# Rounding the narrow SBUF tiles of a float32 transformer kernel up to whole lines of 64 bytes

## Chip, core and metric

The kernel runs on one core of a Trainium2 chip. The metric is the device time of one execution in microseconds.

## The reference

Two blocks of two layers each run over one sequence of 512 tokens with 1024 features, all in float32. The first block is a Fox attention layer (16 heads of 64, a forget gate as a bias) and an MLA attention layer (16 heads, low-rank queries, keys and values), each followed by a gated FFN with a short convolution. The second block is an NSA layer (compressed, selected and window attention, with a multiscale pool beside them) and a conformer convolution of 31 taps, each followed by a SwiGLU FFN. A norm stands ahead of each layer, a residual after it.

```python
def conv_ffn(h, w_in, conv_w, conv_b, w_out):
    u = h @ w_in                                   # 1024 -> 2 * 2816
    u = conv_b + sum(up[:, j:j + s_len] * conv_w[j] for j in range(CONV_W))
    gate, val = jnp.split(u, 2, axis=-1)
    return (jax.nn.silu(gate) * val) @ w_out       # 2816 -> 1024

def first_block(x, ...):
    for layer in range(DEPTH):
        x = x + (fox_mixer(...) if layer < N_A else mla_mixer(...))
        x = x + conv_ffn(rmsnorm(x, ffn_norm[layer]), ...)
    return rmsnorm(x, final_norm)

def second_block(x, ...):
    for layer in range(DEPTH):
        h = rmsnorm_2(x, mix_norm[layer])
        x = x + (nsa_pool_mixer(h, ...) if layer % 2 == 0 else conformer_conv(h, ...))
        x = x + swiglu(rmsnorm_2(x, ffn_norm[layer]), ...)
    return rmsnorm_2(x, final_norm)
```

## The kernel before

Activations lie with features on the partitions and the 512 tokens along the free axis, in chunks of 128 features. The tensor engine multiplies in `float32r`, which keeps only part of a float32, so every factor is split into `hi` and `lo` (`split`, L300): ScalarE writes `hi`, VectorE the rest. A product is then three matmuls, hi with hi, lo with hi and hi with lo (`mm3`, L320 to L323). Most have 128 stationary columns of weights and stream 512 tokens.

Weights are loaded by `load` (L307): 512 KB or less into a `raw` tile of 1024 floats per partition, split at once into tiles `hi` and `lo`; each of the three has three buffers in the pool `wp`. The operand that streams past the weights is `xs` (the split input of a stage, `xsh` and `xsl`, which the MLA also uses for its heads' output), or `hh`/`hl` (the hidden layer of an FFN), `qlh`/`qll` and `lath`/`latl` (the latents of the MLA), `xkh`/`xkl` (a second split input of the MLA), `oh`/`ol` (the heads' output in Fox and NSA) and `poh`/`pol` (the pool's output).

A gated FFN (`ffn`, L692) has two halves: 44 tiles that stream `xs` against `w_in`, and 8 tiles with 22 chunks each that stream `hh` and `hl` against `w_out`. There are four of these. In the attentions a pipeline over heads (`pipeline`, L549) is mixed with projections that are drawn from a queue of generators (`_Fill`). The conformer gives its 31 taps to TensorE, VectorE and GpSimd.

Tiles are allocated from pools that stand one after another in a partition's memory: `cp` (constants: `vecs`, `ident`, `ones`, `gg`, `mhalf`), `wp` (weights), `xp` (`x`, `xs`), `tp` (temporaries, among them `var` twice and `m2`), `rp` (`rt` twice, `r`), and then, each from the same address, the pools of the stages. A stage's pool is released tile by tile, and a later tile waits for those that lay at its place. Tiles are placed in the order in which they are asked for, and each takes a whole number of units of 32 bytes per partition: a tile of 4 floats (`NQ`), such as `var`, takes one unit.

Of the kernel before, what the change touches and what calls it, by code (L numbers as in the profile page):

```python
# [17 lines left out]
P = 128  # L18
T = 512
# [21 lines left out]
def _blocks(w, col_sets):  # L41
    """[K, M] -> [blocks, 128, K/128 * cols]: one contiguous piece for each load."""
    k = w.shape[0] // P
    r = w.reshape(k, P, w.shape[1])
    return np.ascontiguousarray(
        np.stack([r[:, :, c].transpose(1, 0, 2).reshape(P, -1) for c in col_sets])
    )
# [12 lines left out]
def _lay_out(i):  # L60
    """Only layout of the inputs, and constants of the shapes."""
# [147 lines left out]
class _Fill:  # L209
    """Tensor engine work that may stand between the steps of an attention, in order."""  # L210
# [7 lines left out]
    def push(self, name, gen, at=None, gate=None):  # L218
        """gate: (step of the heads, how many heads must be past it), for tiles that are used again."""
        self.q.insert(len(self.q) if at is None else at, (name, gen, gate))  # L220
# [22 lines left out]
    def need(self, name):  # L243
        """The task of this name, to its end."""
        for task in [t for t in self.q if t[0] == name]:
            self._all(task[1])
            self.q.remove(task)
# [7 lines left out]
def _body(ctx, tc, a, out):  # L255
# [14 lines left out]

    nvec = a["vecs"].shape[1]
    vecs = cp.tile([P, nvec], F32, name="vecs")
# [15 lines left out]
    gg = cp.tile([P, NC8], F32, name="gg")  # L288
    G.memset(ones, 1.0)
    mhalf = cp.tile([P, NQ], F32, name="mhalf")  # L290
# [9 lines left out]
    def split(hi, lo, src, scale=None):  # L300
        """hi + lo is src (times scale) to float32's precision; each is exact in float32r."""
        if scale is None:
            return S.copy(hi, src), V.tensor_sub(lo, src, bc(hi))  # L303
        return (S.activation(hi, src, AF.Copy, scale=scale),
                V.scalar_tensor_tensor(lo, src, scale, bc(hi), op0=OP.mult, op1=OP.subtract))  # L305
# [19 lines left out]
    def mm2(acc, w, rh, rl, first, last):  # L325
        """w: hi and lo beside each other, 64 columns each; their products are added by join()."""
        PE.matmul(acc, w, rh, start=first, stop=False)
        PE.matmul(acc, w, rl, start=False, stop=last)
# [8 lines left out]
    def lin(acc, w, act, ks, cols, first=True, last=True, w0=0):  # L337
        """acc[cols, tokens] += sum over the chunks ks of w[k][:, cols].T @ act[k]."""
        wh, wl = w
        ah, al = act  # L340
        for n, k in enumerate(ks):
            mm3(acc, wh[:, k - w0, cols], wl[:, k - w0, cols], ah[:, k], al[:, k],
                first and n == 0, last and n == len(ks) - 1)
            yield STEP
# [8 lines left out]
    class Stats:  # L353
        """Sum over features of squares, gathered chunk by chunk."""
# [26 lines left out]
    def rsqrt(dst, src, n, eps):  # L381
        v = tp.tile([P, NQ], F32, name="var", tag="var", bufs=2)
        V.tensor_scalar(v, src, 1.0 / n, eps, op0=OP.mult, op1=OP.add)
        G.tensor_tensor(dst, v, mhalf, op=OP.pow)

    def wide(r):
        """[128 tokens, 4] -> the same for every partition, [128, 512]."""
        pr = bank("pr")
        for i in range(NQ):
            PE.transpose(pr[:, sl(i)], r[:, i : i + 1].to_broadcast([P, P]), ident)  # L390
        return pr
# [6 lines left out]
    class Norm:  # L398
        """Reciprocal root mean square of the tokens. What is made of it waits until the tensor
        engine has other work in hand: evictions that need it are put off by after()."""  # L400
# [7 lines left out]
        def step(self):  # L408
            if self.t is None:
                self.t = self.pool.tile([P, NQ], F32, name=self.name + "t", tag=self.name + "t", bufs=2)  # L410
                self.square(self.t)
            elif self.b is None:
                self.b = spread(self.t, self.pool, self.name)
                for f in self.put_off:
                    f()
                self.put_off = []
# [4 lines left out]
        def tick(self):  # L421
            """A tile of products has been queued."""
            self.left -= 1
            if self.left <= 0:
                self.step()
# [16 lines left out]
    def split_x(gname, dst=None, st=None, square_on=None):  # L442
        """x times its gain, as hi and lo."""
        dst = dst or xs
        for c in range(NC8):
            last = split(dst[0][:, c], dst[1][:, c], x[:, c], vec(gname, c))
            if st is not None:
                st.add(x[:, c], square_on)
        return last
# [9 lines left out]
    def out_proj(name, act, nk, per, blocks, b0=0, k0=0, late=False):  # L459
        """x += act @ weights; with late, the last chunk of act comes in after all others."""  # L460
        ah, al = [z[:, k0 : k0 + nk] for z in act]
        for b in range(0, blocks, 2):
            tiles = []
            for bb in (b, b + 1):
                w = load(a[name][b0 + bb], nk)
                for m in range(per):
                    tiles.append((bank(), w, sl(m), bb * per + m))
                    if not late:
                        acc = tiles[-1][0]
                        yield from lin(acc, w, (ah, al), range(nk), sl(m))  # L470
                        add_x(bb * per + m, acc)
            if late:
                for ks in (range(nk - 1), range(nk - 1, nk)):
                    for acc, w, cols, m in tiles:
                        yield from lin(acc, w, (ah, al), ks, cols, ks[0] == 0, ks[-1] == nk - 1)
                        if ks[-1] == nk - 1:
                            add_x(m, acc)
# [3 lines left out]
    def stack_q(f, s, name, pool):  # L481
        """Head s of a pair: hi in its own half of the partitions, lo in the other half."""
# [5 lines left out]
    def stack_k(f, s, ka, kl):  # L488
        """hi in both halves of ka, lo in the own half of kl."""
        S.copy(ka[own[s]], f[own[s]])  # L490
        V.tensor_copy(ka[own[1 - s]], f[own[s]])
        V.tensor_sub(kl[own[s]], f[own[s]], bc(ka[own[s]]))

    class Head:
        """Softmax attention of one head in three steps: scores, transposes, values."""
# [4 lines left out]
        def scores(self):  # L500
            pool = self.pool
            nm = pool.tile([P, NQ], F32, name="nm", tag="nm", bufs=3)
            sm = pool.tile([P, NQ], F32, name="sm", tag="sm", bufs=3)
# [10 lines left out]
            rc = pool.tile([P, NQ], F32, name="rc", tag="rc", bufs=3)  # L514
# [34 lines left out]
    def pipeline(prep, n, fill, edge):  # L549
        """Heads in a pipeline, with other work of the tensor engine between their steps."""  # L550
# [21 lines left out]
    # ------------------------------------------------------------------ Fox  # L572
    def fox():
        with ExitStack() as es:
# [27 lines left out]
            def forget():  # L602
# [4 lines left out]
                # softplus(z) with z = -logit: max(z, 0) + ln(1 + exp(-|z|))  # L607
# [83 lines left out]
    # ------------------------------------------------------------- gated FFN  # L691
# [44 lines left out]
    # ------------------------------------------------------------------ MLA  # L736
# [158 lines left out]
    # ------------------------------------------------------------------ NSA  # L895
    def nsa():
        with ExitStack() as es:
# [10 lines left out]
            ccmp = kp.tile([P, NQ * 32 + NQ], F32, name="ccmp")  # L908
# [9 lines left out]
            # two norms in a row: of x, and of what comes of it  # L918
# [8 lines left out]
            r1 = kp.tile([P, NQ], F32, name="r1")  # L927

            def square(t):
                rsqrt(r1, st1.sums(), D, EPS)  # L930
                m2 = tp.tile([P, NQ], F32, name="m2", tag="m2")
# [12 lines left out]
            with phase("n_x") as pool:  # L944
                # compressed keys and values
# [160 lines left out]
            # compressed branch  # L1106
# [82 lines left out]
    # ------------------------------------------------------------ conformer  # L1189
    def conformer():  # L1190
        with ExitStack() as es:
# [9 lines left out]
            with phase("c_x") as pool:  # L1201
# [3 lines left out]
                wdh = pool.tile([P, nw], F32R, name="wdh")  # L1205
                wdl = pool.tile([P, nw], F32, name="wdl")
# [3 lines left out]
                def conv(j, z, on, n_pe):  # L1210
                    """31 taps of chunk j: the first n_pe by the tensor engine, the rest by vector or gpsimd."""
                    y = zc[:, j]
                    if n_pe:
                        zh = pool.tile([P, T + 30], F32R, name="zh", tag="zh", bufs=2)
                        zl = pool.tile([P, T + 30], F32R, name="zl", tag="zl", bufs=2)
# [14 lines left out]
                # layer norm: sums about the mean of three chunks, and the exact shift from it  # L1230
# [88 lines left out]
                def beside(gen):  # L1319
                    """Tensor engine work, with the others' share of the convolutions beside it."""  # L1320
# [35 lines left out]
            rt = pool.tile([P, NQ], F32, name="lnt")  # L1356
            dt = pool.tile([P, NQ], F32, name="lndt")
            d2 = pool.tile([P, NQ], F32, name="lnd2")
# [30 lines left out]
    def final(gname):  # L1389
# [11 lines left out]
        rt = rp.tile([P, NQ], F32, name="rt", tag="rt", bufs=2)  # L1401
# [39 lines left out]
```

## Time and profile before

| | |
|---|---|
| time, median of 3 runs | 2606.76 us (2606.7 to 2606.8) |
| span of the profiled execution | 2603.5 us, 31317 instructions |
| granted clock of TensorE, mean over the span | 0.985 |
| HBM traffic | 83 GB/s over the span |

The span reaches from the first to the last instruction; the run's time also holds what lies around it, 3.3 us by the median. Matmuls are pipelined, so one starts before the one ahead of it ends: the time that a matmul costs in a stream is the distance from one start to the next, which the timeline shows, and not its own duration. Names stand without buffer numbers: `acc<-hh,hi` is a matmul into the accumulator `acc` that streams `hh` against the weights `hi`.

### The profile page before, as it was taken

Reading aid. Unit: us, or ns where it says so; the run is one execution under the profiler, and the core shown is the slowest. Engines: PE = TensorE matmul, PEld = TensorE weight load, DVE = VectorE, ACT = ScalarE, POOL = GpSimd, SP = SyncE. Lnnn points to the kernel's source line nnn. Section 1 sums busy time; section 2 is a strip of 40 time slices with the busy share of each in tenths; the row PEclk is TensorE's granted clock in tenths of the full one; section 3 lists DMA queues with packets and bytes.
Section 4 is the critical chain, followed back from the end, with each engine's and each line's share of the span. In section 5 each row is a group of like instructions: output and inputs, shape, how many; then the busy total and the mean of one; then the engine's idle time right before and its main releaser. Section 6 shows DMA issues by size and latency. Waiting matters only on the chain. (4 is left out here: it accounts for less than half of the span.)

```text
span 2603.5 us, 31317 instructions
## 1 busy us (share of the span) xinstructions
PE 2526.1 (97%) x11903; PEld 2088.6 (80%) x11903; DVE 1627.3 (63%) x2495; ACT 1140.7 (44%) x1933; POOL 464.8 (18%) x369
## 2 busy tenths in 40 slices
PE   8999999999999999999999999999999778999998
PEld 6988888888888888888888888888887546888886
DVE  7887777625677656777436996444328996544422
ACT  4664444324566544444324684222225453333221
POOL 3452000001132212000011222000004763100001
PEclk9999999999999999999999999999999988999999
DMA  4122333333311222333333212333332101333332
GB/s 150 58 66 68 103 97 97 91 97 102 88 57 55 72 73 83 102 96 95 93 93 117 64 51 84 97 97 96 89 100 73 57 17 33 99 97 97 93 97 69
DMA packets 65447, 218.90 MB, mean 84 GB/s; under 512 B 7536, under 2 KB 8560, under 8 KB 65296
## 3 DMA queue, kind: packets, MB, share of 16 engines
q1 hardware_dynamic: 65296, 216.90, 27.1%
q8 instruction: 93, 1.52, 0.3%
q14 instruction: 58, 0.48, 0.1%
HBM read 214.70 MB, written 2.10 MB: 83 GB/s over the span
## 5 line engine op out<-in xcount | busy, mean ns | idle before, releaser
L303 ACT CAST hi<-raw 128x1024 fp32r<-128x1024 f32 (+4 forms) x417 | 420.5, 1010 | 919.5 <-PE acc L322 716.2
L323 PE MATMUL acc<-xsh,lo 128*128 128x512 f32 x1792 | 700.3, 391 | 15.7 <-DVE lo L303 15.7
L321 PE MATMUL acc<-xsh,hi 128*128 128x512 f32 x1792 | 699.6, 392 | 3.0 <-ACT xsh L303 2.9
L303 DVE TENSOR_TENSOR lo<-raw,hi 128x1024 fp32r<-128x1024 f32 (+4 forms) x417 | 499.8, 1199 | 322.8 <-ACT hi L303 317.7
L322 PE MATMUL acc<-xsl,hi 128*128 128x512 f32 x1792 | 700.5, 391 | 0.8 <-DVE xsl L305 0.8
L323 PEld LDWEIGHTS acc<-xsh,lo 128*128 128x128 f32 x1792 | 338.2, 189 | 88.9 <-DVE lo L303 18.7
L321 PEld LDWEIGHTS acc<-xsh,hi 128*128 128x128 f32 x1792 | 338.2, 189 | 73.6 <-ACT xsh L303 3.3
L322 PEld LDWEIGHTS acc<-xsl,hi 128*128 128x128 f32 x1792 | 338.0, 189 | 73.1 <-DVE xsl L305 2.1
L373 POOL TENSOR_TENSOR ssum<-ssum,sq 128x512 f32<-128x512 f32 x75 | 120.4, 1609 | 1482.3 <-ACT sq L367 1472.3
L321 PE MATMUL acc<-hh,hi 128*128 128x512 f32 x704 | 279.1, 396 | 0.0
L322 PE MATMUL acc<-hl,hi 128*128 128x512 f32 x704 | 279.1, 396 | 0.0
L323 PE MATMUL acc<-hh,lo 128*128 128x512 f32 x704 | 279.1, 396 | 0.0
L522 POOL TENSOR_SCALAR lg<-lg,rc 128x384 f32<-128x384 f32 (+3 forms) x144 | 165.8, 1167 | 384.2 <-DVE rc L515 300.6
L710 DVE TENSOR_TENSOR y<-acc,r 128x512 f32<-128x512 f32 x88 | 60.4, 691 | 219.7 <-PE acc L323 219.5
L457 DVE TENSOR_TENSOR x<-x,acc 128x512 f32<-128x512 f32 x104 | 70.6, 685 | 158.6 <-PE acc L323 158.3
L323 PEld LDWEIGHTS acc<-hh,lo 128*128 128x128 f32 x704 | 132.6, 188 | 32.3
L322 PEld LDWEIGHTS acc<-hl,hi 128*128 128x128 f32 x704 | 132.6, 188 | 32.3
L321 PEld LDWEIGHTS acc<-hh,hi 128*128 128x128 f32 x704 | 132.6, 188 | 32.3
L1285 POOL TENSOR_TENSOR zc<-zc,pr 128x496 f32<-128x496 f32 (+17 forms) x79 | 127.0, 1611 | 65.2 <-ACT pr L1281 56.7
L707 DVE SCALAR_TENSOR_TENSOR y<-u,vecs,y 128x510 f32<-128x510 f32 (+1 forms) x176 | 130.9, 748 | 3.4 <-ACT y L705 0.6
L512 ACT ACTIVATE lg<-lg,nm 128x128 f32<-128x128 f32 x192 | 107.1, 560 | 47.2 <-DVE nm L510 46.3
L303 ACT CAST hh<-y 128x512 fp32r<-128x512 f32 x88 | 54.6, 621 | 135.6 <-DVE y L714 135.6
(366 smaller groups left out, 3843.1 us busy)
## 6 DMA issues: line engine op xcount, KB each, us to landing
raw<-in_ffn_in SPq DMA_DIRECT2D x88, 512.0 KB
raw<-in_swi_in SPq DMA_DIRECT2D x88, 512.0 KB
raw<-in_ffn_out SPq DMA_DIRECT2D x32, 448.0 KB
raw<-in_swi_out SPq DMA_DIRECT2D x32, 448.0 KB
raw<-in_pw SPq DMA_DIRECT2D x24, 512.0 KB
raw<-in_fox_qk SPq DMA_DIRECT2D x16, 512.0 KB
raw<-in_ffn_out SPq DMA_DIRECT2D x16, 512.0 KB
raw<-in_uqk SPq DMA_DIRECT2D x16, 512.0 KB
```

Source lines behind the costliest of these rows:

```text
L303: return S.copy(hi, src), V.tensor_sub(lo, src, bc(hi))
L321: PE.matmul(acc, lh, rh, start=first, stop=False)
L322: PE.matmul(acc, lh, rl, start=False, stop=False)
L323: last_mm[0] = PE.matmul(acc, ll, rh, start=False, stop=last).ins
L373: (sum_on or G).tensor_add(self.s, self.s, sq)
L457: V.tensor_add(x[:, c], x[:, c], acc)
L512: S.activation(lg, lg, AF.Exp, bias=nm[:, i : i + 1], scale=-1.0, accum_out=sm[:, i : i + 1])
L522: (V if i in self.on_v else G).tensor_scalar(self.p[i], self.p[i], rc[:, i : i + 1], None, op0=OP.mult)
L707: V.scalar_tensor_tensor(y[:, sh:], u[:, : T - sh], vec(f"cw{l}{2 - sh}", jj), y[:, sh:], op0=OP.mult, op1=OP.add)
L710: V.tensor_mul(y, acc, norm.b)
L1285: G.tensor_add(y[:, sh:], y[:, sh:], pr[:, sh:])
```

## The change

A helper `narrow` allocates a tile whose width is rounded up to a multiple of 16 floats and hands out the part that is used. All tiles of 4 or 8 floats and the others whose width isn't a multiple of 16 are allocated by it. Instructions, loops and transfers stay the same. Comments and docstrings are also blanked; after the new helper all lines stand 4 lower.

```diff
+    def narrow(pool, n, dt=F32, **kw):
+        return pool.tile([P, -(-n // 16) * 16], dt, **kw)[:, :n]
...
-    vecs = cp.tile([P, nvec], F32, name="vecs")
+    vecs = narrow(cp, nvec, name="vecs")
...
-    gg = cp.tile([P, NC8], F32, name="gg")
+    gg = narrow(cp, NC8, name="gg")
-    mhalf = cp.tile([P, NQ], F32, name="mhalf")
+    mhalf = narrow(cp, NQ, name="mhalf")
...
-        v = tp.tile([P, NQ], F32, name="var", tag="var", bufs=2)
+        v = narrow(tp, NQ, name="var", tag="var", bufs=2)
...
-                self.t = self.pool.tile([P, NQ], F32, name=self.name + "t", tag=self.name + "t", bufs=2)
+                self.t = narrow(self.pool, NQ, name=self.name + "t", tag=self.name + "t", bufs=2)
...
-            nm = pool.tile([P, NQ], F32, name="nm", tag="nm", bufs=3)
-            sm = pool.tile([P, NQ], F32, name="sm", tag="sm", bufs=3)
+            nm = narrow(pool, NQ, name="nm", tag="nm", bufs=3)
+            sm = narrow(pool, NQ, name="sm", tag="sm", bufs=3)
...
-            rc = pool.tile([P, NQ], F32, name="rc", tag="rc", bufs=3)
+            rc = narrow(pool, NQ, name="rc", tag="rc", bufs=3)
...
-            ccmp = kp.tile([P, NQ * 32 + NQ], F32, name="ccmp")
+            ccmp = narrow(kp, NQ * 32 + NQ, name="ccmp")
...
-            r1 = kp.tile([P, NQ], F32, name="r1")
+            r1 = narrow(kp, NQ, name="r1")
...
-                m2 = tp.tile([P, NQ], F32, name="m2", tag="m2")
+                m2 = narrow(tp, NQ, name="m2", tag="m2")
...
-                wdh = pool.tile([P, nw], F32R, name="wdh")
-                wdl = pool.tile([P, nw], F32, name="wdl")
+                wdh = narrow(pool, nw, F32R, name="wdh")
+                wdl = narrow(pool, nw, name="wdl")
...
-                        zh = pool.tile([P, T + 30], F32R, name="zh", tag="zh", bufs=2)
-                        zl = pool.tile([P, T + 30], F32R, name="zl", tag="zl", bufs=2)
+                        zh = narrow(pool, T + 30, F32R, name="zh", tag="zh", bufs=2)
+                        zl = narrow(pool, T + 30, F32R, name="zl", tag="zl", bufs=2)
...
-            rt = pool.tile([P, NQ], F32, name="lnt")
-            dt = pool.tile([P, NQ], F32, name="lndt")
-            d2 = pool.tile([P, NQ], F32, name="lnd2")
+            rt = narrow(pool, NQ, name="lnt")
+            dt = narrow(pool, NQ, name="lndt")
+            d2 = narrow(pool, NQ, name="lnd2")
...
-        rt = rp.tile([P, NQ], F32, name="rt", tag="rt", bufs=2)
+        rt = narrow(rp, NQ, name="rt", tag="rt", bufs=2)
```

## Rows read from the trace of the kernel before

**Rows 1.** The page, busy us of each engine (share of the span) xinstructions

```profile
PE 2526.1 (97%) x11903; PEld 2088.6 (80%) x11903; DVE 1627.3 (63%) x2495; ACT 1140.7 (44%) x1933; POOL 464.8 (18%) x369
```

**Rows 2.** Windows: stretch, its us, busy us by engine, granted clock, DMA

```profile
256.00:496.00 240.00, 240.00 (x1066) 198.82 (x1065) 177.91 (x224) 111.49 (x139) 8.54 (x5) 1.00 0.31 97
496.00:622.00 126.00, 126.00 (x540) 101.35 (x539) 41.06 (x45) 34.87 (x43) 10.12 (x8) 1.00 0.33 95
...
700.00:960.00 260.00, 260.00 (x1421) 225.47 (x1420) 179.76 (x375) 148.54 (x322) 64.85 (x60) 1.00 0.21 65
...
1962.00:2168.00 206.00, 158.08 (x599) 119.45 (x597) 198.81 (x232) 106.23 (x198) 129.09 (x82) 0.89 0.13 42
```

**Rows 3.** Timeline of PE, an FFN's first half: start us, duration us, what

```profile
299.81 0.39 PE L323 MATMUL acc<-xsh,lo 128*128 128x512 f32 x1
...
301.85 0.39 PE L323 MATMUL acc<-xsh,lo 128*128 128x512 f32 x1
```

**Rows 4.** Timeline of PE, an FFN's second half

```profile
539.64 0.39 PE L322 MATMUL acc<-hl,hi 128*128 128x512 f32 x1
...
542.92 0.39 PE L321 MATMUL acc<-hh,hi 128*128 128x512 f32 x1
```

**Rows 5.** Timeline of PE, the MLA's low-rank projections

```profile
652.52 0.39 PE L322 MATMUL acc<-xsl,hi 128*128 128x512 f32 x1
...
655.01 0.40 PE L321 MATMUL acc<-xkh,hi 128*128 128x512 f32 x1
...
656.88 0.40 PE L323 MATMUL acc<-xkh,lo 128*128 128x512 f32 x1
```

**Rows 6.** Timeline of PE, MLA attention, an output projection that streams xs

```profile
864.79 0.39 PE L323 MATMUL acc<-xsh,lo 128*128 128x512 f32 x1
...
870.68 0.40 PE L321 MATMUL pq<-qlh,hi 128*128 128x512 f32 x1
```

**Rows 7.** Timeline of PE, MLA, a query projection that streams ql

```profile
673.11 0.40 PE L321 MATMUL pq<-qlh,hi 128*128 128x512 f32 x1
...
677.33 0.95 PE L378 MATMUL pst<-ones,ssum 128*128 128x1 f32 x8
```

**Rows 8.** Groups by line, engine, operation and shape, of PE: xcount, busy us, mean ns

```profile
L322 PE MATMUL acc<-xsl,hi 128*128 128x512 f32 x1792 | 700.5, 391 | 0.8 <-DVE xsl L305 0.8
...
L321 PE MATMUL acc<-hh,hi 128*128 128x512 f32 x704 | 279.1, 396 | 0.0
...
L321 PE MATMUL pq<-qlh,hi 128*128 128x512 f32 x144 | 58.3, 405 | 0.0
...
L321 PE MATMUL acc<-oh,hi 128*128 128x512 f32 x96 | 38.0, 401 | 0.2 <-DVE nm L510 0.2
```

**Rows 9.** Waits, whole span: who waited for whom, us, times, longest

```profile
ACT hi L303 <- PE acc L322: 716.2, 262, 9.4
```

**Rows 10.** Timeline of PE, an FFN's first half after an interruption

```profile
268.46 0.40 PE L322 MATMUL acc<-xsl,hi 128*128 128x512 f32 x1
...
270.54 0.39 PE L322 MATMUL acc<-xsl,hi 128*128 128x512 f32 x1
```

**Rows 11.** Timeline of PE, MLA, values from lat, 256 columns

```profile
684.25 0.28 PE L321 MATMUL pv<-hi,lath 128*128 128x256 f32 x1
...
687.12 0.40 PE L321 MATMUL pq<-qlh,hi 128*128 128x512 f32 x1
```

**Rows 12.** Timeline of PE, Fox, values from xs, 256 columns

```profile
30.77 0.28 PE L322 MATMUL pv<-lo,xsh 128*128 128x256 f32 x1
...
34.13 0.28 PE L322 MATMUL pv<-lo,xsh 128*128 128x256 f32 x1
```

**Rows 13.** Groups by line of DVE: x is aligned, y is not

```profile
L457 DVE TENSOR_TENSOR x<-x,acc 128x512 f32<-128x512 f32 x104 | 70.6, 685 | 158.6 <-PE acc L323 158.3
L710 DVE TENSOR_TENSOR y<-acc,r 128x512 f32<-128x512 f32 x88 | 60.4, 691 | 219.7 <-PE acc L323 219.5
```

## Prediction

> **What bounds the kernel now.** I read the page's busy line first. The tensor engine is busy for 97% of the span, far ahead of the others [rows 1]. I then cut the span by stage with the table of windows. In a gated FFN's first half (256 to 496 us), in its second half (496 to 622) and in the MLA attention (700 to 960) the tensor engine is busy for the whole window, so what its matmuls save there moves the end. In the conformer (1962 to 2168) it is busy for 158 of 206 us and the vector engine for 199; there the vector engine sets the pace [rows 2].
>
> A matmul's own duration says little here, since matmuls overlap. What counts is the distance from one start to the next, and the timeline gives it. In the middle of an FFN's first half ten rows in a row go from 299.81 to 301.85, nine distances of 226.7 ns [rows 3]. In its second half fifteen rows go from 539.64 to 542.92, fourteen distances of 234.3 ns [rows 4]. Both are 128x512, with weights from the same buffers, at a granted clock of 1.00, the higher of its two levels [rows 2]; nothing idles between them. The difference is 7.6 ns, 3%.
>
> What differs is the streamed operand. The addresses in the program of before follow from its allocations: every tile takes whole units of 32 bytes per partition. The weights (`raw`, `hi`, `lo`), `x` and `xs` start on multiples of 64. Then come narrow tiles of one such unit (`var` twice, `m2`, `rt` twice), an odd number, and the pools of the phases start at 119,200, which is 32 past a multiple of 64. So `hh`, `hl`, `qlh`, `lath`, `oh`, `poh` and `xkh` are 32 off, `xs` is not.
>
> The cleanest place to see it is one loop of one stage. At 655.01 the low-rank projections of the MLA go on from `xs` to `xk`, with all else alike: eleven distances before it average 226.4 ns, eight after it 233.8 [rows 5]. The attention stage is no explanation either: there, a run of 26 on `xs` keeps 226.5 [rows 6], and 18 on `ql` take 234.4 [rows 7].
>
> **The change part by part.** No instruction, transfer or loop is added, removed or moved; tiles grow. `gg` and `mhalf` each grow by one unit of 32, which moves weights, `x` and `xs` by 64; `var`, `m2` and `rt` grow by five units, so the phases start at 119,424 = 1866 x 64. The narrow tiles inside the phases (`nm`, `sm`, `rc`, `rqt`, `ccmp`, `r1`, `wdh`, `wdl`, `lnt`) are rounded as well, so all later tiles stay on the multiple. The fullest phase ends at 228,096 before and 576 bytes later after, which still fits. Tiles of one phase wait for tiles of the phase before that lay at the same place. They shift together by at most some hundred bytes, and the few neighbours that are gained or lost (`ph` against `qf` in the NSA) are the heads' tiles, free before the last output projection. I cost that at nothing: the projection's last 96 matmuls, 22 us at 227 ns, cover it, and without them a phase's first tiles would wait that long at most.
>
> Costs, with 226.7 for an aligned stream and 234.3 for one that is off:
>
> FFN second half. `hh` and `hl` give 3 x 704 = 2112 matmuls [rows 8], in unbroken streams: 2112 x 7.6 ns = 16.1 us. The weights' splits don't hinder it: ScalarE's split waits 716 us in total for the tensor engine to free a buffer [rows 9], so it is ahead, and the first half eats the same bytes per matmul at 226.7 already. If that cover were gone, this term would be zero.
>
> MLA. `qlh` and `qll` 3 x 144 [rows 8], and `lat`, by the code 2 chunks x 16 heads x 3 = 96: 528 matmuls. They are interrupted by short ones. After an interruption even an aligned stream starts slowly: nine distances average 231.1 ns [rows 10] before it falls to 226.7. A run of 18 then averages 228.9, and one that is off 234.4 [rows 7]: 5.5 at best. Parts are broken up more often, so I take 4.5: 2.4 us. Bounds: 0, if no run is long enough, and 528 x 7.7 = 4.1.
>
> Output projections and `xk`. `oh`, `ol` 3 x 96 [rows 8], `po` 96 and `xk` 72 by the code: 456 matmuls, half in streams, half between heads. At 5 ns 2.3 us; bounds 0 and 3.5.
>
> Scores and values at 512 columns: 256 matmuls in runs of two to five, some with the weights' side off. I take 2 ns, 0.5 us; bounds 0 and 256 x 7.6 = 1.9.
>
> Narrower ones cost nothing: with the stationary side off (`lath`) 24 matmuls of 256 columns take 119.6 ns each [rows 11], with both aligned 28 take 120.0 [rows 12].
>
> The conformer's 222 convolution matmuls slide by 4 bytes per tap and wait for the vector engine: nothing. For the other engines the nearest pair is an add into `x` (aligned), 685 ns, and a multiply into `y` (off), 691 [rows 13]: at most 0.9%, which on the conformer's 199 us of VectorE is 1.7 us. I take zero for the sum and keep 1.7 for the low end.
>
> Sum: 16.1 + 2.4 + 2.3 + 0.5 = 21.3 us. The profiled span is 2603.5 us; the median of the runs is 2606.76, so 3.3 us lie around it, and the change doesn't touch them. Span 2582.2, time 2585.5.
>
> [...]
>
> **The rivals.**
>
> *The place, not the line.* All tiles that are off also lie above 119,200, and nearly all aligned streams below. If the 7.6 ns came from the distance to the weights or from the upper region, a shift of 224 bytes changes nothing: 2606.8. For it: the two are confounded in the rows, and in the narrow matmuls alignment shows no effect. Against it: the size. 16 of 512 columns take 7.1 ns of 226.7, and 16 columns of float32 are 64 bytes: just one line more, where a row of 2048 bytes starts off its line and needs 33 in place of 32.
>
> *Half of it.* The line counts, but so does where the stream stands against the weights. After the change `hh` starts on a multiple of 128 and the weights 64 off one; before, `xs` and the weights shared their place. If that leaves half the excess, the gain is 10.7 us: 2596.
>
> *Slower: a line of 128.* The 64 bytes that `gg` and `mhalf` add move `xs`, `hi` and `lo` from a multiple of 128 (xs 73,984 = 578 x 128) to 64 off. For it: the two offsets in the rows are not alike; `xk` (96 past a multiple of 128) takes 233.8, `hh` (32 past) 234.3 [rows 4, 5]. Against it: 128 bytes are 32 columns, 14 ns by the same share, and the step seen is half of that. Price: the `xs` streams are 3 x 1792 [rows 8] and some 450 in the Fox heads, 5830; at 7.6 ns 44 us are lost, and the 21.3 are still gained: 2630. It decides from 3.7 ns per `xs` matmul on (21.3 us over 5830).
>
> **How the numbers follow.** The forecast has 0.62, half of it 0.13, no effect 0.14, slower 0.11. The time is the forecast's, 2585.5; its own range is 2580 (all 3352 matmuls at 7.7 ns, 25.8 us, and most of the 1.7) to 2592 (the FFN's 16.1 less a tenth). Forecast and half together hold 0.75, so the range for 8 in 10 has to reach no effect: 2580 to 2608. A measurement of this kernel tells about 0.2% (5 us) from no change: faster 0.75, same 0.14, slower 0.11.
>
> **What would show it.** In the profile after: `hh` streams at 226.7 from start to start, an FFN's second half (528 matmuls) 4.0 us shorter; the MLA 2 to 4 us shorter; FFN first halves unchanged; the conformer unchanged. Wrong would be: `hh` still at 234 (place), 230 (half), `xs` above 227 (a longer line), or a new wait at a phase's start.

## The result, and the profile after

The changed kernel takes 2589.88 us (median of 4 runs, 2588.97 to 2592.52), the one before 2606.78 us (4 runs, 2606.7 to 2608.59). The ratio is 0.9936, with a 95% interval of 0.9922 to 0.995. That is 16.9 us faster where 21.3 was forecast; the time lies inside the range of 2580 to 2608, which held no change as well, 4.4 us above the forecast of 2585.5.

The page of the kernel after, its span and the busy line that answers to [rows 1]:

```profile
span 2588.1 us, 31317 instructions
PE 2512.7 (97%) x11903; PEld 2088.8 (81%) x11903; DVE 1626.9 (63%) x2495; ACT 1141.1 (44%) x1933; POOL 467.1 (18%) x369
```

All five counts are those of before, and every engine but the tensor engine is busy within 0.5% as long. The tensor engine lost 13.4 us of busy time, the span 15.4 us (2603.5 to 2588.1). The medians differ by 1.5 us more than the spans: the prediction had read 3.3 us between before's profiled span and its median, but in seven later executions of before, and in the four of after, 1.8 us lie around the span, so that first profiled execution was probably some 1.5 us shorter than the median.

Windows of after, the stretches of [rows 2]:

```profile
256.00:496.00 240.00, 240.00 (x1067) 198.87 (x1066) 177.16 (x223) 110.81 (x139) 7.92 (x5) 1.00 0.31 98
496.00:622.00 126.00, 126.00 (x552) 103.38 (x551) 44.90 (x48) 38.75 (x48) 12.14 (x9) 1.00 0.34 101
700.00:960.00 260.00, 260.00 (x1443) 227.03 (x1442) 182.44 (x382) 148.68 (x324) 66.28 (x61) 1.00 0.20 64
```

The busy time of the tensor engine fills each window as before; what changes is how many matmuls fit: 1067 for 1066 in an FFN's first half, 552 for 540 in its second, 1443 for 1421 in the MLA. The windows are fixed in time, so a few of these are work that moved up from later.

The timeline of PE gives the distances. All means here and below are taken from the starts in whole ns that the trace holds; the rows shown round a start to 10 ns, so over a short run they can give a mean that is about 1 ns off. (In whole ns the prediction's short means of 226.4, 233.8 and 231.1 are 226.6, 233.6 and 231.8 [rows 5, 10].) First an FFN's second half from end to end: the first and the last of its 528 matmuls on `hh` and `hl`, in the kernel before:

```profile
497.24 0.40 PE L321 MATMUL acc<-hh,hi 128*128 128x512 f32 x1
...
620.70 0.39 PE L323 MATMUL acc<-hh,lo 128*128 128x512 f32 x1
```

and in the kernel after:

```profile
496.22 0.40 PE L325 MATMUL acc<-hh,hi 128*128 128x512 f32 x1
...
616.86 0.39 PE L327 MATMUL acc<-hh,lo 128*128 128x512 f32 x1
```

527 distances take 123.46 us before, 234.3 ns each, as in [rows 4]; they take 120.64 us after, 228.9 ns each. The other three second halves take the same two times to 0.01 us. So `hh` got faster, but stands 2.2 ns above `xs`, which kept its 226.7 ns (16 distances of after, answering to [rows 3]):

```profile
298.79 0.39 PE L327 MATMUL acc<-xsh,lo 128*128 128x512 f32 x1
...
302.42 0.39 PE L325 MATMUL acc<-xsh,hi 128*128 128x512 f32 x1
```

And in the MLA's low-rank projections of after, the place of [rows 5]:

```profile
648.03 0.39 PE L326 MATMUL acc<-xsl,hi 128*128 128x512 f32 x1
...
651.20 0.39 PE L325 MATMUL acc<-xkh,hi 128*128 128x512 f32 x1
...
656.57 0.39 PE L327 MATMUL acc<-xkh,lo 128*128 128x512 f32 x1
```

Fourteen distances on `xs` average 226.6 ns, the 23 on `xk` 233.3, hardly less than before's 233.6. Yet `xk` now starts on a multiple of 64 like everything else. With every operand on a multiple of 64 bytes there are three speeds: 226.7, 228.9 and 233.3 ns.

Where the 15.4 us came from, cut at the first and last `hh` matmul of each FFN (us, worked out from the timelines):

```
                                       before    after    gain   forecast
start, Fox, FFN 1 first half           497.24   496.22    1.0    }
MLA and FFN 2 first half               627.96   624.45    3.5    } 5.2
NSA and FFN 3 first half               461.18   460.77    0.4    }
conformer and FFN 4 first half         507.74   508.02   -0.3    }
after the last hh                       15.57    16.11   -0.5    }
four FFN second halves (528 each)      493.85   482.56   11.3    16.1
```

### The profile page after: what moved, and what is told of

It reads as the page before. It is cut to its first block, busy times and chain, and to the rows that moved or that the text cites. A ratio compares the mean times of both kernels' runs of the same rounds, so it can differ in the third digit from the quotient of the medians.

```text
span 2588.1 us, 31317 instructions
## 1 busy us (share of the span) xinstructions
PE 2512.7 (97%) x11903; PEld 2088.8 (81%) x11903; DVE 1626.9 (63%) x2495; ACT 1141.1 (44%) x1933; POOL 467.1 (18%) x369
## 5 line engine op out<-in xcount | busy, mean ns | idle before, releaser
L326 PE MATMUL acc<-hl,hi 128*128 128x512 f32 x704 | 273.2, 388 | 0.0
```

The costliest lines, as they stand in the source:

```text
L326: PE.matmul(acc, lh, rl, start=False, stop=False)
```

## The experiments

From here on, a distance is one of addresses; the time from one start to the next is called a step. Three theories stood after the result. L, the line: the start of the stream within a line of 64 bytes counts, and something smaller besides it. R, the distance: what counts is where the streamed operand starts relative to the weights (their addresses' difference modulo a few hundred bytes), whatever either's alignment. E: the extra needs other engines' traffic on the memory. By the allocations `hi` and `lo` stand at one place modulo 512, and the distances from them are: `xs` 0 before and after; `hh` 160 before and 320, which is 64 modulo 256, after (the weights moved by 64, the phases by 224); `xk` 224 before and 448 (192) after, since the rounded tiles ahead of it in its phase move it by 64 more.

**map: every distance, the tensor engine alone.** One kernel loads once, splits once and then runs groups of 48 matmuls of the kernel's form (hi·hi, lo·hi, hi·lo), with the stream moved by 16 bytes at a time (`MOFF`: 0, 4, to 124 floats) and the weights at 0, 32 and 128 past a multiple of 512 (`WOFF`: 0, 8, 32 floats). The core of the edit:

```diff
+    for n, w0 in enumerate(WOFF):
+        for m, m0 in enumerate(MOFF):
...
+                    wa, wb = [w[:, w0 + k * P : w0 + (k + 1) * P] for w in (wh, wl)]
+                    ma, mb = [z[:, m0 + k * T : m0 + (k + 1) * T] for z in (mh, ml)]
...
+                    PE.matmul(acc, wa, ma, start=first, stop=False)
+                    PE.matmul(acc, wa, mb, start=False, stop=False)
+                    PE.matmul(acc, wb, ma, start=False, stop=last)
```

> This kernel leaves the whole model out. It measures the disputed cost by itself: nothing runs but TensorE, in the kernel's own order (hi with hi, hi with lo of the other side, lo with hi), 512 columns, new weights for each matmul, 48 matmuls for each of 32 offsets of the streamed operand (0 to 496 bytes in steps of 16), and that for weights at 0, 32 and 128 bytes past a multiple of 512. Theory L (line): a stream whose operand starts on a multiple of 64 takes 226.7 ns per matmul, any other 233 to 237, whatever the weights' offset; eight offsets of 32 are fast. Theory R (distance): what counts is the distance from the weights' address to the streamed operand's within some period up to 512 bytes; with the weights at 0 the kernel's own rows give 226.7 at distance 0, 229.0 at 320, 234.3 at 160, 233 at 224 and 448; with the weights moved by 32 or 128 the same pattern moves along. Theory E (other engines): the extra 2 to 8 ns are collisions with ScalarE, VectorE or DMA, and with those idle all offsets give 226.7.

Timeline of PE, the 17th and the last of the 48 matmuls of six groups. In the accumulators' names the first letter is the place of the weights (a 0, b 32, c 128), the last two the stream's offset in steps of 16, in base 8 (aa 0, ac 32, ba 128, bc 160, ce 320):

```profile
22.93 0.39 PE L291 MATMUL wa_maa__77<-ml,wh 128*128 128x512 f32 x1
...
29.96 0.39 PE L292 MATMUL wa_maa__77<-mh,wl 128*128 128x512 f32 x1
...
131.14 0.39 PE L291 MATMUL wa_mbc__567<-ml,wh 128*128 128x512 f32 x1
...
138.41 0.40 PE L292 MATMUL wa_mbc__567<-mh,wl 128*128 128x512 f32 x1
...
242.48 0.39 PE L291 MATMUL wa_mce__1057<-ml,wh 128*128 128x512 f32 x1
...
249.57 0.39 PE L292 MATMUL wa_mce__1057<-mh,wl 128*128 128x512 f32 x1
...
376.26 0.40 PE L291 MATMUL wb_maa__1645<-ml,wh 128*128 128x512 f32 x1
...
383.50 0.40 PE L292 MATMUL wb_maa__1645<-mh,wl 128*128 128x512 f32 x1
...
398.28 0.39 PE L291 MATMUL wb_mac__1743<-ml,wh 128*128 128x512 f32 x1
...
405.31 0.39 PE L292 MATMUL wb_mac__1743<-mh,wl 128*128 128x512 f32 x1
...
821.85 0.39 PE L291 MATMUL wc_mba__3605<-ml,wh 128*128 128x512 f32 x1
...
828.88 0.39 PE L292 MATMUL wc_mba__3605<-mh,wl 128*128 128x512 f32 x1
```

31 steps each: 226.7 ns at distance 0, 234.3 at 160, 228.9 at 320. With weights 32 off, a stream on a multiple of 512 takes 233.4, and one that is 32 off as well takes 226.7. With weights at 128 it is the stream at 128 that takes 226.7. All three sets laid over each other by distance modulo 256 (ns, median of the six groups at each):

```
distance   0     16    32    48    64    80    96    112
ns       226.7 231.6 233.3 233.4 228.9 231.0 233.3 231.3
distance  128    144   160   176   192   208   224   240
ns       232.3 233.3 234.3 233.3 233.4 234.6 233.4 226.7
```

Of the 96 groups 94 lie within 0.3 ns of this; one at 64 and one at 128 took 233.4 and 233.5, so the distance doesn't settle all. L falls: the fast place moves with the weights. E falls: nothing else runs, and distance 160 takes 234.3 all the same. R holds, with a period of 256, and it gives the kernel's figures: 160 for `hh` before (234.3), 64 after (228.9), 224 and 192 for `xk` (233.4 both).

**all32: the whole layout moved by 32 bytes.** One narrow tile more in `cp`: `xs` and weights lose their multiple of 64, `hh` gains it, no distance changes.

```diff
+    cp.tile([P, 8], F32, name="pad")
```

> The kernel before with one unused tile of 32 bytes after the constants: weights, x, xs and all phases move together by 32, so xs, hi and lo are 32 off a multiple of 64, and hh, ql, lat and oh are on one; all distances stay. Theory L: the 5830 xs matmuls rise from 226.7 to 234 ns (44 us), the others fall by 16 to 21 us: 2630. Theory R: xs stays at 226.7 and hh at 234.3: 2606.8, within 3 us.

2607.01 us in one run, between the before's 2605.18 and 2608.73 on that chip (7 runs; before was run again beside each set of experiments). Timeline of all32, `xs` (14 steps) and an FFN's second half (527):

```profile
298.89 0.39 PE L322 MATMUL acc<-xsh,hi 128*128 128x512 f32 x1
...
302.07 0.39 PE L324 MATMUL acc<-xsh,lo 128*128 128x512 f32 x1
...
497.45 0.40 PE L322 MATMUL acc<-hh,hi 128*128 128x512 f32 x1
...
620.92 0.39 PE L324 MATMUL acc<-hh,lo 128*128 128x512 f32 x1
```

226.6 ns off a multiple of 64, 234.3 on one. Alignment to 64 does nothing here, either way.

**dist0: only the phases moved, to distance 0.** The kernel before with 352 bytes more in front of the phases; its narrow tiles stay narrow.

```diff
+    rp.tile([P, 88], F32, name="pad")
```

> The kernel before with one unused tile of 352 bytes in the pool ahead of the phases: hh, ql, lat and Fox's and NSA's oh lie at a multiple of 512 bytes from the weights, and on a multiple of 64; the narrow tiles inside the phases stay as they were. Theory R: hh streams at 226.7, 16 us off the four FFN second halves and 3 to 5 us off the rest: 2586 to 2588, some 3 us below the changed kernel's 2589.9. Theory L: the changed kernel's 229.0 on hh is what a 64-byte line gives, so hh takes 229 here too: 2590 to 2592.

Timeline of dist0, an FFN's second half:

```profile
496.91 0.39 PE L321 MATMUL acc<-hh,hi 128*128 128x512 f32 x1
...
616.36 0.39 PE L323 MATMUL acc<-hh,lo 128*128 128x512 f32 x1
```

119.45 us, 226.7 ns each: the 4.0 us per half that the prediction had written down. The kernel takes 2585.65 us (4 runs, 2584.92 to 2587.45), before on this chip 2605.94; ratio 0.9922, interval 0.9905 to 0.9938. That is 0.35 us below the low end of what R expected. One added tile gives all that the change gave, and by the second halves alone 4.8 us more (119.45 for 120.64 us, four times).

**dist448: the same pad, 64 bytes shorter.** `hh` on a multiple of 64, at distance 448 (192); `xk` comes to 0.

```diff
+    rp.tile([P, 72], F32, name="pad")
```

> The same with 288 bytes: hh, ql, lat and oh again start on a multiple of 64, but 448 bytes (of 512) from the weights, where xk lies in the changed kernel, and xk comes to distance 0. Theory L: hh at 227 to 229, 2586 to 2592. Theory R: hh at about 233, a gain of 3 us at most, 2603 to 2606, and xk, which the change left at 233, falls to 226.7.

Timeline of dist448, the second half and then `xk`:

```profile
497.77 0.39 PE L321 MATMUL acc<-hh,hi 128*128 128x512 f32 x1
...
620.74 0.40 PE L323 MATMUL acc<-hh,lo 128*128 128x512 f32 x1
...
655.07 0.39 PE L321 MATMUL acc<-xkh,hi 128*128 128x512 f32 x1
...
658.47 0.39 PE L321 MATMUL acc<-xkh,hi 128*128 128x512 f32 x1
```

`hh` 233.3 ns though it is on a multiple of 64; `xk` 226.7 (15 steps), which the change itself had left at 233.3. 2603.3 us in one run, 2.6 under the median of before on that chip and 1.9 under its lowest run.

**xs192: the changed kernel with the weights' distance to `xs` spoilt.** Every matmul operand that the change puts on a multiple of 64 stays on one.

```diff
+    xp.tile([P, 48], F32, name="pad")
```

> The changed kernel with one unused tile of 192 bytes ahead of x: every matmul operand that was on a multiple of 64 stays on one, hh comes to distance 0 from the weights (modulo 256), xs to distance 192. Theory R: the xs matmuls rise from 226.7 to 233.4 (5830 x 6.7 ns, 39 us), hh falls to 226.7 (5 us): 2620 to 2625, slower than the kernel before. Theory L: 2590.

Timeline of xs192, `xs` and a second half:

```profile
298.74 0.39 PE L327 MATMUL acc<-xsl,hi 128*128 128x512 f32 x1
...
302.47 0.39 PE L328 MATMUL acc<-xsh,lo 128*128 128x512 f32 x1
...
503.60 0.39 PE L326 MATMUL acc<-hh,hi 128*128 128x512 f32 x1
...
623.08 0.39 PE L328 MATMUL acc<-hh,lo 128*128 128x512 f32 x1
```

`xs` takes 233.3 ns (16 steps), `hh`, now at distance 0, 226.7. 2619.43 us in one run: with every operand on a multiple of 64, it is 13.0 us slower than the kernel before on that chip (2606.43, 9 runs). It came 0.6 us below the low end of what R expected.

**best: everything at distance 0.** The changed kernel with seven pads, so that all 512-column operands are congruent modulo 256 (the core of the edit):

```diff
+    rp.tile([P, 48], F32, name="pad")
...
+            kp.tile([P, 32], F32, name="pad")
...
+            kp.tile([P, 48], F32, name="pad2")
```

> The changed kernel with unused tiles (192 bytes ahead of the phases, 64 to 192 after groups of narrow tiles inside them) that put every operand of the 512-column matmuls at a distance of 0 from the other, modulo 256. Theory R: hh from 229.0 to 226.7 (4.9 us), ql, lat, oh, po, xk and the heads' scores and values 2 to 3 us: 2582 to 2584, some 7 us below the changed kernel and 2 to 3 below the kernel with 352 bytes. Theory L: all operands already lie on lines of 64, nothing changes: 2590.

2584.95 us (5 runs, 2584.66 to 2586.42) beside 2606.43 for before, ratio 0.9919, interval 0.9905 to 0.9933; expected were 2582 to 2584, so it missed by 1 us. That is the fastest kernel here, but against dist0 (2585.65) within the spread of the runs. Its second halves take 119.45 us, as in dist0. Shorter runs don't reach 226.7: `ql` and `xk` average 228.6 and 228.4, `poh` 230.3, the values at 512 columns 228.6 (232.4 before) and the scores 231.6 (231.0 before, when more than half of them stood at distance 0 already). And one group got slower: the MLA's 192 value matmuls of 256 columns, whose stationary operand is `lat`, take 115.7 ns each after the change and 121.2 here, a loss of 1.1 us. The first 24 of them, up to the matmul that follows, in after:

```profile
680.32 0.28 PE L325 MATMUL pv<-hi,lath 128*128 128x256 f32 x1
...
683.05 0.39 PE L325 MATMUL pq<-qlh,hi 128*128 128x512 f32 x1
```

and in best:

```profile
678.62 0.28 PE L325 MATMUL pv<-hi,lath 128*128 128x256 f32 x1
...
681.49 0.40 PE L325 MATMUL pq<-qlh,hi 128*128 128x512 f32 x1
```

These 24 take 114.0 ns each in after and 119.3 in best; in before they took 119.8 [rows 11].

**map2: which forms of matmul pay.** As map, weights at 0, with 512, 384, 256 and 128 streamed columns and with 64 and 32 stationary ones.

```diff
+KINDS = [(512, 128), (384, 128), (256, 128), (128, 128), (512, 64), (512, 32)]
+MOFF = [0, 8, 16, 24, 32, 40, 48, 56, 60]
...
+                    wa, wb = [w[:, k * P : k * P + rows] for w in (wh, wl)]
+                    ma, mb = [z[:, m0 + k * T : m0 + k * T + cols] for z in (mh, ml)]
```

> The model is left out again: TensorE alone, weights at 0, the streamed operand 0 to 224 bytes further in steps of 32 and 240, 48 matmuls each, for 512, 384, 256 and 128 columns with 128 stationary columns, and for 512 columns with 64 and 32 stationary columns. If the extra is a meeting of the two reads of TensorE (weights and stream), it shrinks with fewer stationary columns: with 32 of them a quarter of the 6.7 ns or less. If it belongs to the stream alone, it stays at 6.7. For narrower streams the kernel's rows saw no effect at 256 columns (120.0 and 119.6): the same 120 at all distances there; 384 columns open.

```
columns x stationary   distance 0   other distances
512 x 128                 226.6     229.0 (64) to 234.3 (160)
384 x 128                 173.3     173.3 (32, 64, 160, 224) to 180.0 (240)
256 x 128                 120.0     117.1 to 120.2
128 x 128                 111.6     111.6 to 111.8
512 x 64                  230.2     226.7 (240), else 228.4 to 232.7
512 x 32                  231.7     228.9 (240) to 233.3
```

Timeline of map2, 512 columns against 32 stationary ones at distance 0 (31 steps, 231.7 ns):

```profile
394.73 0.40 PE L291 MATMUL kf_maa__2282<-ml,wh 128*32 128x512 f32 x1
...
401.92 0.39 PE L292 MATMUL kf_maa__2282<-mh,wl 128*32 128x512 f32 x1
```

Each form has its own pattern. At 128 columns the distance does nothing (0.2 ns). At 256 it counts, but distance 0 is among the slow places, as the value matmuls in best show. A simple picture, in which reading the weights collides with reading the stream, would have the extra shrink with a quarter of the weights; it doesn't: with 32 stationary columns the nine distances take 2.2 to 6.6 ns more than 226.7. With 64 and 32 stationary columns distance 0 is not even the fast place.

## Why the prediction was right about the time, and where it failed

**What bounds the kernel: right.** Where the tensor engine fills its windows, each ns per matmul moved the end: 11.3 us in the FFNs' second halves, 4.1 elsewhere, together the 15.4 of the span. In the conformer, where VectorE sets the pace (busy for 198.8 of 206 us, the tensor engine for 158.1 [rows 2]), nothing moved (-0.3 us). The two speeds that the prediction compared were taken at one clock: the granted clock is 1.00 in the windows of both FFN halves [rows 2]; its lower level in the trace of before, 0.50, stands for example from 1544 to 1546 us.

**The cause: wrong.** The step that failed is the forecast's own premise, that a stream is slow because it starts off its line of 64 bytes; no run shows such a line. It rested on two cases, `xs` and `hh`, that differ in alignment and in distance to the weights at once, and on a coincidence of size (16 extra columns, 7.1 ns, for the 7.6 seen). all32 exchanged the two alignments without exchanging the speeds, and dist448 and xs192 have slow streams on a multiple of 64 (`hh` and `xs`, 233.3 ns each). What the change did to the time came from a side effect: 64 bytes into the weights' place and 224 into the phases' turned a distance of 160 into one of 64, one of the better places by accident (234.3 and 228.9 ns in map). That the time came near the forecast was luck: dist448 has `hh` on a multiple of 64 as well, and gains 2.6 us.

**FFN second half: the term was mis-sized, 16.1 forecast, 11.3 measured.** 2112 matmuls was right; 7.6 ns each was not. `hh` went to 228.9, not to 226.7. dist0, which does bring it to 226.7, ends at 2585.65, beside the forecast of 2585.5 (a gain of 20.3 us for the 21.3): the sum was that of a layout which the change doesn't make.

**The smaller terms: 5.2 forecast, 4.1 measured.** The stretch with the MLA gave 3.5, the one with Fox 1.0, NSA 0.4 and the tail -0.5. By operand, from every matmul's step before and after: `ql` and `lat` gave 2.0 us (forecast 2.4), the output projections and `xk` 1.3 (2.3), the scores and values at 512 columns 0.4 (0.5). `ql` matmuls whose next one starts within 260 ns went from 233.9 to 229.8 on average (forecast 4.5 ns, measured 4.1), `oh` from 234.0 to 229.6 (5 and 4.4). `xk` was wrong: distance 224 became 192, and it stayed at 233.

That narrow matmuls cost nothing was wrong too. The two cases that it rested on, 119.6 and 120.0 ns [rows 11, 12], stand at distances 96 and 0 (stream against stationary operand), which are alike by accident (120.2 and 120.0 in map2). The change moved the MLA's 192 value matmuls from 96 to 192, and they went from 121.4 to 115.7 ns: 1.1 us that the forecast had put at zero. The other matmuls, none of their groups more than 0.8 us either way, take the remaining 0.7 us back. Two counts were low, without weight: 284 scores, values and others at 512 columns for 256, and 6024 matmuls on `xs` for 5830.

**The covers: right.** ScalarE's split still waits for the accumulators. Waits of after, who for whom, us, times, longest, answering to [rows 9]:

```profile
ACT hi L307 <- PE acc L326: 707.0, 262, 9.6
```

and VectorE's groups, answering to [rows 13], are unchanged to 1 ns, so the 1.7 us kept for them didn't come. No new wait shows at a phase's start either: the span less the tensor engine's busy time is 75.4 us, where it was 77.4. VectorE's groups of after:

```profile
L461 DVE TENSOR_TENSOR x<-x,acc 128x512 f32<-128x512 f32 x104 | 70.5, 684 | 153.5 <-PE acc L327 153.0
L714 DVE TENSOR_TENSOR y<-acc,r 128x512 f32<-128x512 f32 x88 | 60.5, 691 | 219.7 <-PE acc L327 219.5
```

**The rivals.** *Half of it* came nearest. It said that where the stream stands against the weights counts too, and put `hh` at 230; the measured 228.9 lies between it and the forecast, with 71% of the excess gone (5.4 of 7.6 ns). But no run shows a line beside the distance: in all32 `xs` kept its speed off a multiple of 64 (226.6 ns), and `hh` on one (234.3). *The place* had the distance in it. It was set aside for the coincidence of size, and its time put at no change because a shift of 224 bytes (160 against the weights) was thought to change nothing; with the period of 256 in map it does (234.3 ns at 160, 228.9 at 64). *A line of 128* is refuted: `xs` kept 226.7 when it went from 0 to 64 modulo 128.

**What stays open.** Why the distance counts. For 512 columns against 128 the runs show its period (256 bytes), its fast places (0, and 240 in most groups: 226.7 ns), and that no other engine's traffic is needed for it (map, 226.7 to 234.6 ns with the tensor engine alone). The extra doesn't shrink with the number of stationary columns (with 32 of them 2.2 to 6.6 ns over 226.7, in map2), though which distance is fast changes with it. Why a few groups at one distance took another time isn't shown, nor what meets what inside. No run keeps the weights loaded from one matmul to the next, or tests another type than float32r.

## What to carry to other kernels

Two streams of one form at two speeds are worth an address table: take the distance between the streamed operand and the weights, not only each one's alignment, and test one against the other by moving everything together (all32) and by moving one alone (dist0). For float32r matmuls of 512 columns against 128, place the stream and the weights alike modulo 256 bytes (226.7 ns at distance 0 and up to 234.6 elsewhere in map; at 256 columns distance 0 is no fast place, 120.0 ns in map2 where the fastest took 117.1); one pad in front of the phases was worth 20 us of 2606, and the same pad 64 bytes shorter some 2.6. A change that helps is no proof of its reason: the rounding to 64 worked by the distance it happened to leave, and 192 bytes more in one pool made it slower than before.

## What the runs showed of the hardware that was not expected

With the tensor engine alone and nothing to wait for, 512 float32r columns against 128 take 226.7 to 234.6 ns from start to start, by the distance of the operands modulo 256 in 94 of 96 groups. The slow places are no fixed delay but short cycles: in map2 the steps repeat, within 1 ns, 226, 229, 232 ns at distance 64 and 229, 237 at 128, and `hh` of after, at 64, repeats the first three. Something besides the distance counts too, and no run shows what: distance 240 took 226.7 in all six groups of map and 233.3 in map2. And at 256 columns, where 120.0 ns is taken at distance 0, all others but 96 are a little faster (117.1 to 118.6).
